# New addresses for the operands of 14,000 matmuls: odd pitches for the activations, reversed k-tiles for the weights

## The chip, the cores and the metric

One core of a Trainium2 chip runs the whole program. The metric is the time of one execution on the device in microseconds (us), lower is better. Matmuls run on TensorE (PE), whose clock the chip grants at one of two levels, 1.2 or 2.4 GHz.

## The reference, cut to what matters

Two token groups, 128 context tokens and 256 latent tokens, go through one layer of width 2048. All heavy work is a product of the 384 tokens with a weight matrix:

```python
h = rmsnorm(x, norm_mix_g) * (1 + sc_a) + sh_a
z = h @ w_in                              # 2048 x 16944: mLSTM, retention, SSD inputs and gates
merged = g0 * (y_m @ w_br_m) + g1 * (y_r @ w_br_r) + g2 * (y_s @ w_br_s)   # 1024 x 2048 each
x = x + g_a * (merged @ w_out)            # 2048 x 2048
h = rmsnorm(x, norm_mlp_g) * (1 + sc_f) + sh_f
x = x + g_f * (square(relu(h @ w_ff1)) @ w_ff2)        # 2048 x 8192, 8192 x 2048
```

The scans between the products are small beside them. Everything is fp32.

## The kernel before, in words

**Split products.** TensorE takes `float32r`, a rounded fp32. To keep fp32 precision each operand is split into a rounded half and its remainder (`hi`, `lo`), and each product is three matmuls: hi·hi, hi·lo, lo·hi. In a line of the profile such as `gb<-hlo,whi` the first name is the moving operand, which is streamed column by column, the second the stationary one, 128 columns of which are loaded into the array by an LDWEIGHTS ahead of each matmul (PEld).

**Activations.** Their halves have 16 k-tiles of 128 rows by T = 384 tokens, all in SBUF: `hhi`/`hlo` (normalised input, pool `hp`), `yhi`/`ylo` (branch outputs, 8 k-tiles, pool `hl`), `mhi`/`mlo` (merged, pool `mh`), `h2i`/`h2l` (input of the MLP, pool `h2`), `ahi`/`alo` (squared ReLU, pool `pf`). Each half is a tile of its own, and a k-tile follows the one before it at a pitch of 384 words, 1,536 bytes.

**Weights.** `strip` cuts a weight matrix into units of 512 KB. SP loads each into a `raw` tile of 128 x 1024 (6 buffers); `emit_splits` runs three units ahead (`SPB` = 3): `rnd` (ACT, L88) writes `whi`, `tt` (DVE, L91) writes `wlo`. A unit holds four k-tiles of 256 columns, or two of 512 (kind `B5`). `products` issues the matmuls (L100) in three forms: kind `A` streams the activations (384 columns) past the weights, kinds `B2` and `B5` stream the weights (256 and 512 columns) past 128-token slices of the activations. `run_units` goes through the units in order, so the order of all matmuls is fixed by the program; the 32 units of the first stage are split by `st_split` instead.

**Addresses.** In the built program `whi`, `wlo` and `raw` buffers, `hhi`, `hlo`, `h2i`, `h2l`, `mhi`, `mlo`, `yhi`, `ylo`, `ahi` and `alo` all begin 64 bytes past a multiple of 512 bytes (`whi` at 51,776, `hhi` at 76,352, `ahi` at 151,104, `yhi` at 175,168). All pitches are multiples of 512 bytes too. So in every split product the moving and the stationary operand start a multiple of 512 bytes apart. Two tiles that nothing reads, `hpad` (88 words, pool `hl`) and `fpad` (80 words, pool `pf`), take part in that. Other tiles lie otherwise: `Cb` begins 416, `W` 384 and `x2` 480 bytes past a multiple of 512.

Of the kernel before, what the change touches and what calls it, by code (L numbers as in the profile page):

```python
# [9 lines left out]
F32R = mybir.dt.float32r  # L10
# [5 lines left out]
D = 2048  # L16
T = 384
KT = D // 128
DFF = 8192
EPS = 1e-6  # L20
MQ, MK, MV, MO, MI = 0, 1024, 2048, 3072, 4096
# [25 lines left out]
def hybrid_step(ctx: ExitStack, tc: tile.TileContext, cpack, x_prompt, x_sample, c, state_mlstm_C,  # L47
# [24 lines left out]
    hp = Pool("hp")  # L72
    P = {}

    def bank(name="sb"):
        return psum([128, 512], name, bufs=4, tag="s")

    def gbank(name="gb"):
        return psum([128, 512], name, bufs=4, tag="g")
# [4 lines left out]
    def r3(ap, a):  # L84
        return ap.rearrange("p (a b) -> p a b", a=a)

    def rnd(out, in_, **kw):
        act.activation(out=out, in_=in_, func=AF.Copy, **kw)  # L88

    def tt(eng, out, a, b, op):  # L90
        eng.tensor_tensor(out=out, in0=a, in1=b, op=op)  # L91
# [7 lines left out]
    def mm(out, l, r, start=True, stop=True):  # L99
        pe.matmul(out, l, r, start=start, stop=stop)  # L100

    def tp(out, in_):
        n = in_.shape[0]
        pe.transpose(out, in_, ident[0:n, 0:n])
# [3 lines left out]
    raws, splits, done = {}, {}, set()  # L108
# [5 lines left out]
    def strip(w, c0, kt, operand, evac, kind="A", row0=0, post=None, pre=None, sync=False, hold=0):  # L114
# [3 lines left out]
        for k0 in range(0, kt, uk):  # L118
# [4 lines left out]
            if mods and tune["due"] >= 1:  # L123
                m = mods.popleft() + (tune["mx"],)
                tune["due"] -= 3 if m[2] == 7 else 1
                raw_list.append((mod_src(*m[:3]), 2))
                unit_list.append((Block("M", m, None, KT), len(raw_list) - 1, 0, 1))

    def raw_done(i):
        done.add(i)  # L130
        while pos["used"] in done:
            done.discard(pos["used"])
            pos["used"] += 1

    def emit_raws():
        while pos["raw"] < min(len(raw_list), pos["used"] + RAWB):
            src, nk = raw_list[pos["raw"]]
            t = raw_tile()
            sp.dma_start(out=r3(t, nk), in_=src)
            raws[pos["raw"]] = t  # L140
            pos["raw"] += 1

    def emit_splits(n):
        while pos["split"] < min(n, len(unit_list)):
            i = pos["split"]
            blk, ri, k0, uk = unit_list[i]
            emit_raws()
            while ri not in raws:
                pop_mods(1)
                emit_raws()  # L150
            if blk.kind != "M":
                s = raws.pop(ri)
                hi = strm([128, 1024], "whi", bufs=SPB, dt=F32R)
                lo = strm([128, 1024], "wlo", bufs=SPB, dt=F32R)
                rnd(hi, s)
                tt(dve, lo, s, hi.bitcast(F32), ALU.subtract)
                splits[i] = (r3(hi, uk), r3(lo, uk))
                raw_done(ri)
            pos["split"] += 1

# [92 lines left out]
    def K(n):  # L253
        o, s = CW[n]
        return cp[:, o:o + s] if o < CW1 else P["cr"][:, o - CW1:o - CW1 + s]
# [35 lines left out]

    cs = cst([128, KT, 32], "cs")
    pool.memset(cs, 0.0)
# [30 lines left out]
    def mod_src(m, q, r):  # L324
        o = m * D + 512 * q
        return w_mod[0, 256 * r:256 * r + 256, o:o + 512].rearrange("(k p) f -> p k f", p=128)
# [58 lines left out]
    def gf_load(q):  # L385
        if "gf" not in P:
            waiting.append(q)
            return
        ready.add(q)
        for v in range(2):  # L390
            sp.dma_start(out=P["gf"][:, v, 512 * q:512 * q + 512],
                         in_=scr_mod[1, v, 512 * q:512 * q + 512].partition_broadcast(128))

    def pop_mods(n):
        while half:
            half.pop()()
        while n and dq:
            f = dq.popleft()
            if f is None:
                break  # L400
            f()
            n -= 1
# [4 lines left out]
    rst = start([128, 3], "rst")  # L407
    acc = start([128, KT, T], "acc")
    graw = start([128, KT, 48], "graw")
    scr_g = dram([3 * KT, 128, T], "scr_g")  # L410
    junk = acc.rearrange("p k t -> p (k t)")
# [3 lines left out]
    dve.reciprocal(out=rst, in_=rst)  # L415

    scA, shA, scF, shF = (cst([128, KT, 2], n) for n in ("scA", "shA", "scF", "shF"))
    hhi = hp([128, KT, T], "hhi", dt=F32R)
    hlo = hp([128, KT, T], "hlo", dt=F32R)
    groups = [(k, 1) for k in range(4)] + [(k, 2) for k in range(4, KT, 2)]  # L420
    NG = len(groups)
    todo, mraw, wraw, wsp, mps = deque(), {}, {}, {}, {}
# [152 lines left out]
    i = 0  # L575
# [628 lines left out]
    def r_evac_v(p):  # L1204
        def f(ps):
            t = P["r"]([128, 3, 256], "vtok", bufs=2)
            src = r_tok(ps)
            for c_ in range(3):
                act.copy(out=t[:, c_], in_=src[c_])
            heads[p]["v"] = t  # L1210
            bg.append(r_scan(p))
        return f

    def r_scan(p):
# [30 lines left out]
        for hh in range(2):  # L1245
# [31 lines left out]
            for d in range(2):  # L1277
                for a, c_ in ((0, 0), (1, 1 + d)):
                    i = 2 * a + d
# [27 lines left out]
        for hh in range(2):  # L1307
            i = 2 * p + hh
# [2 lines left out]
                tp(p_[:, 128 * c_:128 * c_ + 128], o[:, hh, 128 * c_:128 * c_ + 128])  # L1311
            RR[i] = P["hl"]([128, T], "y_r", tag="ylo%d" % i)
            act.activation(out=RR[i], in_=p_[:, 0:T], func=AF.Copy, scale=gr[:, i:i + 1])
        if p == 3:
            P["hl"]([128, 88], "hpad")
        yield

    def y_split(i, src):
# [143 lines left out]
    def turn(k, p):  # L1462
        for v, a, b in GRP:
            act.activation(out=P["xa"][:, k, a:b], in_=p[:, a:b], func=AF.Copy, scale=scF[:, k, v:v + 1])
# [9 lines left out]
    def o_last(ps):  # L1474
        x2, ga, o, r = P["x2"], P["ga"], P["o"], P["r2"]
        q = slice(1536, D)
        act.activation(out=r, in_=r, func=AF.Sqrt)
        tb = [gbank(), gbank(), bank(), bank()]
        rbp = bank()
        dg = o([128, 3, 128], "dg2")  # L1480

        def close_tokens(i):
            t = o([128, 512], "to", bufs=3)
            tt(dve, t, ps[i], ga[:, min(i, 1), q], ALU.mult)
            tt(dve, x2[:, i, q], x2[:, i, q], t, ALU.add)
            act.activation(out=t, in_=x2[:, i, q], func=AF.Square, accum_out=P["sso"][:, i, 3:4])
            for j in range(4):
                tp(tb[j][:, 128 * i:128 * i + 128], x2[:, i, 1536 + 128 * j:1664 + 128 * j])

        for i in range(3):  # L1490
            close_tokens(i)
        dve.tensor_reduce(out=r, in_=P["sso"], axis=mybir.AxisListType.X, op=ALU.add)
        act.activation(out=r, in_=r, func=AF.Sqrt, scale=1.0 / D, bias=K("eps")[:, 0:1])
        dve.reciprocal(out=r, in_=r)
        for i in range(3):
            dve.tensor_scalar(out=dg[:, i], in0=ident, scalar1=r[:, i:i + 1], scalar2=None, op0=ALU.mult)
            mm(rbp[:, 128 * i:128 * i + 128], ones, dg[:, i])
        for j in range(4):
            turn(12 + j, tb[j])
        rb = o([128, T], "rb")  # L1500
        P["mh"].close()
        P["h2"] = Pool("h2", "left")
        hi = P["h2i"] = P["h2"]([128, KT, T], "h2i", dt=F32R)
        lo = P["h2l"] = P["h2"]([128, KT, T], "h2l", dt=F32R)
        xa = P["xa"]

        def make(ks):
            for k in ks:
                if k > 1 and k % 4:
                    tt(pool, xa[:, k], xa[:, k], rb, ALU.mult)  # L1510
                else:
                    tt(dve, xa[:, k], xa[:, k], rbp[:, 0:T], ALU.mult)
                for v, a, b in GRP:
                    act.activation(out=hi[:, k, a:b], in_=xa[:, k, a:b], func=AF.Identity, bias=shF[:, k, v:v + 1])  # L1514
                if k == 0:
                    act.copy(out=rb, in_=rbp[:, 0:T])
                for v, a, b in GRP:
                    dve.scalar_tensor_tensor(out=lo[:, k, a:b], in0=xa[:, k, a:b], scalar=shF[:, k, v:v + 1],  # L1518
                                             in1=hi[:, k, a:b].bitcast(F32), op0=ALU.add, op1=ALU.subtract)

        def rest():
            make(range(6, 10))
            yield
            make(range(10, 14))
            yield
            make(range(14, 16))
            o.close()
            P["f"] = Pool("pf", "right")
            P["gf"] = P["f"]([128, 2, D], "gf")
            for n in waiting:  # L1530
                gf_load(n)
            P["ahi"] = P["f"]([128, KT, T], "ahi", dt=F32R)
            P["alo"] = P["f"]([128, KT, T], "alo", dt=F32R)
            P["ssf"] = P["f"]([128, 3, 4], "ssf")
            P["rf"] = P["f"]([128, 3], "rf")
            P["f"]([128, 80], "fpad")
            dve.memset(P["rf"], 1.0)
            yield

        make(range(2))  # L1540
        emit_splits(pos["split"] + 1)
        make(range(2, 6))
        bg.append(rest())

    for n in range(4):
# [165 lines left out]
```

## Time and profile before

| what | value |
|---|---|
| time, median of 2 runs | 2836.24 us (2834.62 to 2837.87) |
| time of the profiled execution | 2840.32 us |
| its span, first to last instruction | 2838.2 us |
| mean granted TensorE clock | 0.989 of full |
| PE busy | 2760.8 us, 97% |
| DVE, ACT, POOL busy | 55%, 41%, 27% |
| DMA | 52.8% of 16 engines' span |

A matmul's own duration in the profile (338 ns for 384 columns) is a latency: the next one starts long before it ends. What counts is the time from one matmul's start to the next one's, which is read from the timeline or from the chain.

### The profile page before, as it was taken

How to read it: one execution, taken by the hardware profiler on the slowest of the kernel's cores; microseconds unless marked ns; L12 is line 12 of the kernel's file. 1: busy time of each engine (PE TensorE's matmuls, PEld its weight loads, DVE VectorE, ACT ScalarE, POOL GpSimd, SP SyncE). 2: the span in 40 equal slices, each digit the busy share in tenths (PEclk: the TensorE clock that was granted, in tenths of full speed). 3: DMA queues.
4: the chain of work that ended last, by engine and by line, in shares of the span. 5: the costliest groups of instructions: out<-in, count | busy, mean ns of one | idle time of the engine just before them, and what ended most of it. 6: DMA issues, size and time to landing. Idle time of an engine off the chain costs nothing. (4 is left out here: it accounts for less than half of the span.)

```text
span 2838.2 us, 40379 instructions
## 1 busy us (share of the span) xinstructions
PE 2760.8 (97%) x16167; PEld 2584.6 (91%) x16167; DVE 1551.8 (55%) x1871; ACT 1153.4 (41%) x1723; POOL 777.7 (27%) x608
## 2 busy tenths in 40 slices
PE   6999999999999999999999998999999999999998
PEld 5899998898999999999999877998899899889987
DVE  3666656555555445576877855873343344334434
ACT  5333444446443344444444545552233233323333
POOL 3200333422333222145676633341100110010012
PEclk9999999999999999999999999999999999999999
DMA  9955565454545445476656563664444444444443
GB/s 313 300 193 167 157 176 147 149 156 137 171 131 166 139 135 151 144 224 203 190 179 193 191 217 127 183 198 139 127 126 128 132 127 126 127 133 127 126 141 104
DMA packets 387284, 461.23 MB, mean 163 GB/s; under 512 B 19668, under 2 KB 302952, under 8 KB 385944
## 3 DMA queue, kind: packets, MB, share of 16 engines
q1 hardware_dynamic: 387096, 458.65, 52.8%
q8 instruction: 127, 2.08, 0.3%
q14 instruction: 61, 0.50, 0.1%
HBM read 446.19 MB, written 12.40 MB: 162 GB/s over the span
## 5 line engine op out<-in xcount | busy, mean ns | idle before, releaser
L91 DVE TENSOR_TENSOR wlo<-raw,whi 128x1024 fp32r<-128x1024 f32 x599 | 820.8, 1375 | 968.9 <-ACT whi L88 953.6
L88 ACT ACTIVATE whi<-raw 128x1024 fp32r<-128x1024 f32 x600 | 632.6, 1059 | 961.8 <-PE gb L100 494.5
L100 PE MATMUL gb<-hhi,whi 128*128 128x384 f32 x1600 | 555.0, 347 | 14.6 <-ACT whi L88 5.4
L100 PE MATMUL gb<-hhi,wlo 128*128 128x384 f32 x1600 | 543.5, 340 | 8.8 <-DVE wlo L91 8.7
L100 PE MATMUL gb<-hlo,whi 128*128 128x384 f32 x1600 | 541.6, 338 | 0.0
L91 POOL TENSOR_TENSOR macc<-macc,raw 128x512 f32<-128x512 f32 x206 | 352.5, 1711 | 331.8 <-issue 259.9
L100 PE MATMUL gb<-h2l,whi 128*128 128x384 f32 x1024 | 344.7, 337 | 4.6 <-DVE h2l L1518 4.5
L100 PE MATMUL gb<-h2i,whi 128*128 128x384 f32 x1024 | 344.2, 336 | 1.6 <-ACT h2i L1514 1.6
L100 PE MATMUL gb<-h2i,wlo 128*128 128x384 f32 x1024 | 343.8, 336 | 0.6 <-DVE wlo L91 0.6
L100 PEld LDWEIGHTS gb<-hhi,whi 128*128 128x128 f32 x1600 | 305.9, 191 | 29.9 <-issue 10.3
L343 DVE SCALAR_TENSOR_TENSOR macc<-raw,cs,macc 128x512 f32<-128x512 f32 x306 | 316.2, 1040 | 5.8
L100 PEld LDWEIGHTS gb<-hhi,wlo 128*128 128x128 f32 x1600 | 305.4, 191 | 12.7 <-DVE wlo L91 12.4
L100 PEld LDWEIGHTS gb<-hlo,whi 128*128 128x128 f32 x1600 | 305.4, 191 | 2.1 <-issue 1.4
L91 POOL TENSOR_TENSOR x<-x,t 128x512 f32<-128x512 f32 x45 | 71.7, 1622 | 815.9 <-DVE t L91 815.9
L100 PE MATMUL gb<-whi,hhi 128*128 128x256 f32 x768 | 222.1, 289 | 0.0
L100 PE MATMUL gb<-wlo,hhi 128*128 128x256 f32 x768 | 218.2, 284 | 3.0 <-DVE wlo L91 3.0
L100 PE MATMUL gb<-whi,hlo 128*128 128x256 f32 x768 | 218.0, 284 | 0.0
L100 PEld LDWEIGHTS gb<-h2l,whi 128*128 128x128 f32 x1024 | 193.2, 189 | 7.7 <-DVE h2l L1518 7.6
L100 PE MATMUL gb<-whi,ahi 128*128 128x512 f32 x512 | 199.3, 389 | 0.0
L100 PE MATMUL gb<-whi,alo 128*128 128x512 f32 x512 | 199.2, 389 | 0.0
L100 PE MATMUL gb<-wlo,ahi 128*128 128x512 f32 x512 | 199.2, 389 | 0.0
L100 PEld LDWEIGHTS gb<-h2i,whi 128*128 128x128 f32 x1024 | 193.5, 189 | 2.9 <-ACT h2i L1514 1.8
(407 smaller groups left out, 4153.7 us busy)
## 6 DMA issues: line engine op xcount, KB each, us to landing
raw<-in_w_in_dram SPq DMA_DIRECT2D x264, 512.0 KB
raw<-in_w_ff_dram SPq DMA_DIRECT2D x256, 512.0 KB
raw<-in_w_mod_dram SPq DMA_DIRECT2D x128, 512.0 KB
mraw<-in_w_mod_dram SPq DMA_DIRECT2D x32, 1024.0 KB
raw<-in_w_out_dram SPq DMA_DIRECT2D x32, 512.0 KB
raw<-in_w_br_r_dram SPq DMA_DIRECT2D x16, 512.0 KB
raw<-in_w_br_m_dram SPq DMA_DIRECT2D x16, 512.0 KB
raw<-in_w_br_s_dram SPq DMA_DIRECT2D x16, 512.0 KB
```

Of the source, the lines that this page charges most:

```text
L88: act.activation(out=out, in_=in_, func=AF.Copy, **kw)
L91: eng.tensor_tensor(out=out, in0=a, in1=b, op=op)
L100: pe.matmul(out, l, r, start=start, stop=stop)
L343: dve.scalar_tensor_tensor(out=macc[:, v], in0=t[:, kk], scalar=cs[:, 2 * r + kk, v:v + 1], in1=macc[:, v], op0=ALU.mult, op1=ALU.add)
```

## The change

- `hhi` and `hlo` become the two halves of one tile `hboth` whose k-tiles lie 772 words (3,088 bytes) apart; `hlo` of a k-tile begins 384 words (1,536 bytes) after its `hhi`.
- `h2i`/`h2l` and `ahi`/`alo` likewise become halves of one tile each, at a pitch of 776 words (3,104 bytes), the remainder 388 words (1,552 bytes) after the rounded half.
- `hpad` goes. That moves `yhi` and `ylo` by 352 bytes.
- In `emit_splits` the views of `whi` and `wlo` are reversed over the unit's k-tiles: k-tile 0 is written at the end of the buffer, the last one at its start. ACT's and DVE's instructions now write (and DVE reads `whi`) in four pieces of 256 words (two of 512 for `B5`) with a negative step between pieces. The products use the same views.

Nothing else changes: the matmuls, their operands' values, their order and the DMAs are the same. `mhi`, `mlo` and `fpad` stay.

```diff
+PITCH, LOW = 776, 388
...
                 hi = strm([128, 1024], "whi", bufs=SPB, dt=F32R)
                 lo = strm([128, 1024], "wlo", bufs=SPB, dt=F32R)
+                hi, lo, s = r3(hi, uk)[:, ::-1], r3(lo, uk)[:, ::-1], r3(s, uk)
                 rnd(hi, s)
                 tt(dve, lo, s, hi.bitcast(F32), ALU.subtract)
-                splits[i] = (r3(hi, uk), r3(lo, uk))
+                splits[i] = (hi, lo)
...
-    hhi = hp([128, KT, T], "hhi", dt=F32R)
-    hlo = hp([128, KT, T], "hlo", dt=F32R)
+    hboth = hp([128, KT, 772], "hboth", dt=F32R)
+    hhi, hlo = hboth[:, :, 0:T], hboth[:, :, T:2 * T]
...
-        if p == 3:
-            P["hl"]([128, 88], "hpad")
...
-        hi = P["h2i"] = P["h2"]([128, KT, T], "h2i", dt=F32R)
-        lo = P["h2l"] = P["h2"]([128, KT, T], "h2l", dt=F32R)
+        both = P["h2"]([128, KT, PITCH], "h2b", dt=F32R)
+        hi, lo = both[:, :, 0:T], both[:, :, LOW:LOW + T]
+        P["h2i"], P["h2l"] = hi, lo
...
-            P["ahi"] = P["f"]([128, KT, T], "ahi", dt=F32R)
-            P["alo"] = P["f"]([128, KT, T], "alo", dt=F32R)
+            both = P["f"]([128, KT, PITCH], "ab", dt=F32R)
+            P["ahi"], P["alo"] = both[:, :, 0:T], both[:, :, LOW:LOW + T]
```

## Rows read from the trace of the kernel before

**Rows 1.** The page: busy time by engine, and granted clock in 40 slices.
```profile
PE 2760.8 (97%) x16167; PEld 2584.6 (91%) x16167; DVE 1551.8 (55%) x1871; ACT 1153.4 (41%) x1723; POOL 777.7 (27%) x608
PEclk9999999999999999999999999999999999999999
```

**Rows 2.** Chain that ended last, 2030 to 2310 us: start, length, matmuls merged.
```profile
2037.90 135.91 PE gb L100 x780
2173.81 1.36 PE sb L100 x6
2175.17 2.72 PE gb L100 x12
2177.89 1.36 PE sb L100 x6
```

**Rows 3.** Timeline of PE near 980 us: start, length, one matmul each.
```profile
980.03 0.28 PE L100 MATMUL gb<-whi,hlo 128*128 128x256 f32 x1
...
980.99 0.28 PE L100 MATMUL gb<-wlo,hhi 128*128 128x256 f32 x1
```

**Rows 4.** Timeline of PE near 439 us.
```profile
438.31 0.53 PE L100 MATMUL gb<-hlo,whi 128*128 128x384 f32 x1
...
440.23 0.53 PE L100 MATMUL gb<-hlo,whi 128*128 128x384 f32 x1
```

**Rows 5.** Stretches: length, busy PE, PEld, DVE, ACT, POOL; PEclk, DMA share, GB/s.
```profile
2000.00:2010.00 10.00, 10.00 (x46) 8.29 (x45) 4.03 (x5) 2.74 (x3) 1.71 (x2) 1.00 0.43 135
438.60:440.50 1.90, 1.90 (x7) 1.90 (x7) 1.86 (x3) 0.06 (x1) 0.00 (x0) 0.50 1.07 370
230.00:580.00 350.00, 335.32 (x2027) 318.79 (x2026) 222.55 (x351) 154.72 (x249) 113.88 (x84) 0.98 0.53 152
```

**Rows 6.** Groups by line with shapes, PE: count, busy us, mean ns.
```profile
L100 PE MATMUL gb<-hhi,whi 128*128 128x384 f32 x1600 | 555.0, 347 | 14.6 <-ACT whi L88 5.4 <-ACT at L536 5.3 <-ACT hhi L88 3.3
L100 PE MATMUL gb<-h2l,whi 128*128 128x384 f32 x1024 | 344.7, 337 | 4.6 <-DVE h2l L1518 4.5
L100 PE MATMUL gb<-whi,hhi 128*128 128x256 f32 x768 | 222.1, 289 | 0.0
L100 PE MATMUL gb<-whi,ahi 128*128 128x512 f32 x512 | 199.3, 389 | 0.0
L100 PE MATMUL gb<-yhi,whi 128*128 128x384 f32 x384 | 128.5, 335 | 0.0
L100 PE MATMUL sb<-whi,ahi 128*128 128x512 f32 x256 | 99.6, 389 | 0.0
```

**Rows 7.** Timelines of PE where weights from other tiles are loaded next.
```profile
526.32 0.34 PE L100 MATMUL gb<-hhi,wlo 128*128 128x384 f32 x1
526.50 1.03 PE L100 MATMUL sb<-v,W 128*128 128x257 f32 x4
...
684.04 0.34 PE L100 MATMUL gb<-hhi,wlo 128*128 128x384 f32 x1
684.22 0.33 PE L100 MATMUL sb<-xd,Cb 128*128 128x64 f32 x2
...
1707.66 0.39 PE L100 MATMUL sb<-whi,mlo 128*128 128x512 f32 x1
1707.89 0.27 PE L104 MATMUL sb<-cp,x 128*128 128x128 f32 x1
```

**Rows 8.** Groups by line with shapes, DVE and ACT: the splits and a comparison.
```profile
L91 DVE TENSOR_TENSOR wlo<-raw,whi 128x1024 fp32r<-128x1024 f32 x599 | 820.8, 1375 | 968.9 <-ACT whi L88 953.6 <-DMA raw<-in_w_out_dram 7.1 <-DMA raw<-in_w_in_dram 4.0
L91 DVE TENSOR_TENSOR Cb<-Cb,cbm 128x1024 f32<-128x1024 f32 x12 | 15.1, 1258 | 0.0
L88 ACT ACTIVATE whi<-raw 128x1024 fp32r<-128x1024 f32 x600 | 632.6, 1059 | 961.8 <-PE gb L100 494.5 <-PE sb L100 375.3 <-issue 36.2
```

**Rows 9.** Who waited for whom, PE alone: us in total, times, longest us.
```profile
PE gb L100 <- DVE wlo L91: 17.5, 20, 1.9
PE gb L100 <- DVE h2l L1518: 4.5, 5, 1.8
```

## The prediction, made before the changed kernel was run

> **What bounds the kernel now.** I read the page first. PE is busy 97% of the span and its clock is at the full level in every slice [rows 1]. So time can only come from what a matmul costs. The second view is the chain that ended last, because its pieces give start-to-start times over many matmuls. In the last unbroken first-MLP stage 780 matmuls take 135.91 us; 12 of them have 512 columns, and 18 of those take 4.08 us, so 226.7 ns each; the 768 with 384 columns then take (135.91 - 12 x 0.2267) / 768 = 173.4 ns each [rows 2]. In the timeline, eight matmuls of 256 columns take 0.96 us, 120 ns each [rows 3].
>
> At 2.4 GHz and one column per cycle, 384, 256 and 512 columns take 160.0, 106.7 and 213.3 ns. So every split product costs 13.3 ns more than its stream, whatever its width, and whichever pool its activations lie in: `h2` and `hhi` and `ahi` lie in different places and give the same excess. I next looked where the clock was at its lower level, 1.2 GHz (granted 0.50 from 438.6 to 440.5 us) [rows 5]: six matmuls of 384 columns take 1.92 us there, 320 ns each, and 384 / 1.2 is 320 [rows 4]. The excess is gone. So the 13.3 ns are not a fixed cost of a matmul. Something cannot keep up with a full-speed stream, and what runs beside each stream is the load of the next matmul's weights.
>
> The touched matmuls, three products to each row: 3 x (1600 + 768) on `hhi`/`hlo` = 7,104; 3 x 1024 on `h2` = 3,072; 3 x (512 + 256) on `ahi`/`alo` = 2,304; 3 x 384 on `yhi`/`ylo` = 1,152 [rows 6]. Together 13,632, whose excess is 13,632 x 13.3 = 181 us. This is the only stock from which new addresses can win.
>
> **The change part by part.** *Addresses of the products.* In the kernel before, moving and stationary operand always lie a multiple of 512 bytes apart. After it, the distance modulo 512 is 16k bytes on `hboth`, 32k on the rounded halves and 32k + 16 on the remainders of `h2` and `ahi`, and 352 on `yhi`/`ylo`. The matmuls keep their columns and their count. The trace of before has no split product with any other distance. The nearest rows are split products during which the weights of another tile are loaded, ahead of a plain fp32 matmul: from `W`, 192 bytes off (modulo 512), from `Cb`, 160 off, from `x2`, 96 off. They take 0.18, 0.18 and 0.23 us [rows 7]. Without any excess they would be 0.160, 0.160 and 0.213. So three other distances don't remove the excess; within the view's grain of 0.01 us they leave it or add some: 0.18 - 0.1734 = 6.6 ns, 0.23 - 0.2267 = 3.3 ns. All three are multiples of 32 bytes; an odd multiple of 16 is in no row. The bounds of this term are thus from -181 us (all excess gone) to 13,632 x 6.6 = +90 us. I take 0, since the three rows lie next to the excess of before and none lies near the bare stream.
>
> The same excess in every row and no excess at half clock also fit a load that takes its share of one path into the array each time, whatever the addresses. And the times are the same whether DVE and ACT are busy 40% and 27% [rows 5] or not: other engines' reads and writes, whose addresses run through all distances, leave no mark on 768 matmuls in a row [rows 2].
>
> Here the Trainium skill can be weighed against the trace. "TensorE: Matmul & The Clock Gate", in "Step-by-step: what each phase is for", gives PE two independent read ports, one for the stream and one for the weights. By that no address matters, and the change is worth 0 us. But the same page, under "Wait — 56ns, not 53.3ns?", puts the floor between two warm matmuls at some 2.5 ns; the trace shows 13.3. If the change brought the matmuls down to that floor, the sum would be 13,632 x 10.8 = 147 us less, an estimate from that page. The trace does not say which of the two holds for an odd distance.
>
> *The reversed split.* 568 units (600 less the 32 of the first stage) get an ACT and a DVE instruction in pieces. DVE's product on `Cb`, whose mask is read in eight pieces per instruction, takes 1,258 ns on the mean, the split 1,375 [rows 8]. So pieces cost nothing visible there; below nothing the bound is the same row, 117 ns a unit, 66 us of DVE work off the path. ACT has no such row; the bound above is as much again, 1,059 ns. What hides either is the matmul work of a unit: 24 x 173.4 = 4.2 us, with three units of lead. Should both double, DVE would do 568 x 1.4 us more, 781 us, and ACT 602; in the densest stretch, 230 to 580 us, 350 / 4.2 = 83 units would lift DVE from 223 to 337 of 350 us [rows 5]. Only there would PE begin to wait on `wlo`, on which it waits 17.5 us in the whole span now [rows 9]. I take 0.
>
> *Shared tiles.* An instruction still writes one k-tile of one half. Matmuls read k-tiles of `h2i` while later ones are still being written, with 4.5 us of waiting on `h2l` in total [rows 9], so waits go by region and not by tile, and two halves in one tile add no wait. Were it by tile, those few us would grow by some us once, at the start of each stage. No DMA, queue or semaphore step moves. The pads and pools only shift addresses.
>
> **The sum.** Profiled execution 2840.3 us, change 0. The median of the runs shown is 4.1 us lower, so the forecast is 2836 us. A measurement of this kernel can tell about 2% from no change, 57 us.
>
> **The rivals.**
> *A collision between reads (faster).* Stream and weight load are read at the same time from the same memory. If they collide when both lie on lines of the same parity, 16 bytes a line, and in no other case, the excess falls away where the distance is an odd multiple of 16: half of `hboth` (odd k), 3,552; the `lo` third of `h2`, 1,024; that of `ahi`, 768. That is 5,344 x 13.3 = 71 us: 2769 by the profiled execution, 2765 by the median. For it: the excess is exactly constant where the distance is, and vanishes at half clock. Against it: in this case it needs a distance the trace doesn't have, and 96, 160 and 192 bytes show the excess.
> *The same, wider.* If only a distance of 0 modulo 512 collides, it stays for k = 0 alone: 12,964 matmuls escape, 172 us, 2664 by the median. The three rows speak against that; only that they load for plain fp32 matmuls leaves it open.
> *Slower.* A stream or load that starts off a 64-byte boundary needs one more fetch. In the kernel before no split product does. Afterwards it is three quarters of `hboth` (5,328), two thirds of `h2` (2,048) and of `ahi` (1,536), and all of `yhi`/`ylo` (1,152): 10,064. At the 3.3 ns of the `x2` row that is 33 us, 2869 by the median; at the 6.6 ns of `Cb`, 66 us, 2903. `x2` and `Cb` begin 32 bytes off such a boundary, which speaks for it; `W` begins on one and reads 0.18 too, which speaks against it. From 5.6 ns on it is over 2%.
> *The change does what it says only in form*: every address moves, and nothing depends on it. That is the forecast.
>
> **How the numbers follow.** Forecast (within 15 us of 2836): 0.60. Parity collision: 0.17, 2765, with some spread. Wider collision: 0.10, 2664. Slower: 0.13, of which 0.06 is over 2%. The range holds the forecast, most of the parity case (from 2745 if a little more than odd multiples escape) and the slower case up to 2885: about 0.60 + 0.14 + 0.09 = 0.83. Its own range for the likeliest case is 2825 to 2850. Faster by over 2%: 0.17 + 0.10, less the part of the parity case that falls short of 57 us, so 0.25. Slower by over 2%: 0.06. Within: 0.69.
>
> **What would show it.** In the changed profile, the piece of the chain for the first-MLP stage should again be close to 136 us for 780 matmuls, and a 512-column unit 4.08 us. If reads collide, k-tiles differ: matmuls on odd k of `hboth`, or on `h2l` and `alo`, would start 160 ns and 213 ns apart and the rest 173 and 227. If a boundary costs, `yhi` and `ylo` matmuls, all 32 bytes off, would all be a few ns longer. The split instructions should stay near 1.06 and 1.38 us, and PE's waits on `wlo` near 17 us. The prediction is wrong if an odd multiple of 16 bytes is special, which no row here could show.

## The result, and the profile of the changed kernel

| | before | changed |
|---|---|---|
| median of the runs | 2836.24 us (2834.62 to 2837.87) | 2856.43 us (2855.93 to 2856.93) |
| profiled execution | 2840.32 us, span 2838.2 us | 2855.93 us, span 2854.1 us |
| mean granted clock | 0.989 | 0.992 |

The ratio on record is 1.0068, 95% interval 1.0051 to 1.0084 (it is not exactly the quotient of the two medians, here or below): a small loss of about 20 us, where nothing was forecast. In the changed kernel all line numbers are one higher: the products stand at L101, the splits at L89 and L92.

The page, busy time and granted clock, to be read beside [rows 1]:

```profile
PE 2778.2 (97%) x16167; PEld 2591.8 (91%) x16167; DVE 1549.4 (54%) x1871; ACT 1152.7 (40%) x1723; POOL 777.3 (27%) x608
PEclk9999999999999999999999999999999999999999
```

The counts and the clock's digits are the same, and the mean granted clock is no lower, but PE is busy 17.4 us longer. So the loss lies in what a matmul costs. The chain that ended last, 2030 to 2310 us, shows it; the piece of 780 is the first-MLP stage of [rows 2], the rest of the rows is the second-MLP stage and the start of the next:

```profile
2040.80 137.49 PE gb L101 x780
2178.30 1.39 PE sb L101 x6
2179.69 2.79 PE gb L101 x12
2182.47 1.40 PE sb L101 x6
2183.87 2.81 PE gb L101 x12
...
2308.86 21.21 PE gb L101 x121
```

In the chain of the kernel before, the stage after that begins with this row:

```profile
2301.65 28.45 PE gb L100 x164
```

The 780 matmuls take 137.49 us instead of 135.91, 1.58 us or 2 ns each more. Where a unit of 18 products with 512 columns took 4.08 us every time, they now take 1.39 + 2.79 = 4.18 and 1.40 + 2.81 = 4.21 us: they cost more, and not all the same. From the first row of the stage to the start of the next it is 2308.86 - 2040.80 = 268.06 us, before 2301.65 - 2037.90 = 263.75 (the start of the x780 piece is in [rows 2]). That is 4.3 us more; there are four such pairs of stages, so some 17 us.

The timelines of PE, first in the branch products with `yhi`/`ylo`, which now all lie 352 bytes away; then with 256 columns, beside [rows 3]; then at half clock, beside [rows 4], with the view by windows under it (granted clock 0.50):

```profile
1242.70 0.34 PE L101 MATMUL gb<-ylo,whi 128*128 128x384 f32 x1
...
1245.88 0.34 PE L101 MATMUL gb<-ylo,whi 128*128 128x384 f32 x1
...
977.73 0.28 PE L101 MATMUL gb<-wlo,hboth 128*128 128x256 f32 x1
...
983.80 0.28 PE L101 MATMUL gb<-wlo,hboth 128*128 128x256 f32 x1
...
438.14 0.52 PE L101 MATMUL gb<-hboth,wlo 128*128 128x384 f32 x1
...
439.10 0.52 PE L101 MATMUL gb<-hboth,wlo 128*128 128x384 f32 x1
```

```profile
438.20:440.00 1.80, 1.80 (x7) 1.80 (x6) 1.80 (x3) 0.00 (x0) 0.00 (x0) 0.50 0.84 269
```

18 products of `y` from 1242.70 to 1245.88 us take 176.7 ns each. The same products in the kernel before took 173.3 ns, 21 from the first row to the last:

```profile
1257.43 0.33 PE L100 MATMUL gb<-yhi,wlo 128*128 128x384 f32 x1
...
1261.07 0.33 PE L100 MATMUL gb<-yhi,wlo 128*128 128x384 f32 x1
```

51 products of 256 columns take 6.07 us, 119.0 ns each, a nanosecond less than before. At half clock three products take 0.96 us, 320 ns each, which is their bare stream, as before. So do 70 products of this trace that ran at half clock without a stall, at ten distances from 0 to 144 bytes.

The splits in the groups by line, beside [rows 8], and after them PE's waits, beside [rows 9]:

```profile
L92 DVE TENSOR_TENSOR wlo<-raw,whi 128x1024 fp32r<-128x1024 f32 x599 | 815.6, 1367 | 987.4 <-ACT whi L89 982.9 <-DMA macc<-in_b_mod_dram 3.2
L89 ACT ACTIVATE whi<-raw 128x1024 fp32r<-128x1024 f32 x600 | 632.6, 1059 | 987.8 <-PE gb L101 500.5
```

```profile
PE gb L101 <- DVE wlo L92: 16.7, 18, 1.9
PE gb L101 <- DVE h2b L1519: 4.5, 5, 1.8
```

In pieces and backwards, the splits take 1,367 and 1,059 ns, where they took 1,375 and 1,059, and PE waits no longer for them. None of the loss is there.

**The whole trace.** Since all starts of matmuls are in the trace and all addresses in the built program, the excess over the bare stream can be averaged for every kind of product (start to next start, less columns / 2.4 GHz; more than 45 ns counts as a stall and is left out, and so is the first 84 us). For each I also took the distance from the operand that streams to the weights that are loaded next. In the kernel before that distance is 0 modulo 512 throughout.

```
kind, columns              matmuls  excess ns: before  changed   difference us
ahi/alo, 512                  2304             13.40    18.15       +10.9
hhi/hlo, 384                 ~4400             13.69    15.21        +6.7
h2, 384                      ~3035             13.38    15.40        +6.1
yhi/ylo, 384                  1145             13.34    16.62        +3.8
hhi/hlo, 256                 ~2210             13.19    11.51        -3.7
mhi/mlo, 512 (not moved)       540             14.30    14.35         0.0
```

The sum is +23.8 us, against 20.2 us between the medians. In the two profiled executions the last matmul comes 15.8 us later; there 5.4 us less went to half-clock stretches, 2.4 us less to stalls and 0.8 us less to the other matmuls of the changed kernel, which closes the sum to within a microsecond.

### The profile page after: what moved, and what is told of

It is laid out like the page before. It is cut to its first block, busy times and chain, and to the rows that moved or that the text cites. A ratio compares the mean times of both kernels' runs of the same rounds, so it can differ in the third digit from the quotient of the medians.

```text
span 2854.1 us, 40379 instructions
## 1 busy us (share of the span) xinstructions
PE 2778.2 (97%) x16167; PEld 2591.8 (91%) x16167; DVE 1549.4 (54%) x1871; ACT 1152.7 (40%) x1723; POOL 777.3 (27%) x608
## 5 line engine op out<-in xcount | busy, mean ns | idle before, releaser
L92 DVE TENSOR_TENSOR wlo<-raw,whi 128x1024 fp32r<-128x1024 f32 x599 | 815.6, 1367 | 987.4 <-ACT whi L89 982.9
L89 ACT ACTIVATE whi<-raw 128x1024 fp32r<-128x1024 f32 x600 | 632.6, 1059 | 987.8 <-PE gb L101 500.5
L101 PE MATMUL gb<-hboth,whi 128*128 128x384 f32 x3200 | 841.9, 344 | 14.2 <-ACT at L538 5.2
L101 PEld LDWEIGHTS gb<-hboth,whi 128*128 128x128 f32 x3200 | 582.7, 190 | 31.6 <-issue 12.0
L101 PE MATMUL gb<-hboth,wlo 128*128 128x384 f32 x1600 | 544.9, 341 | 8.5 <-DVE wlo L92 8.5
L101 PE MATMUL gb<-h2b,whi 128*128 128x384 f32 x2048 | 529.9, 339 | 6.2 <-DVE h2b L1519 4.5
L92 POOL TENSOR_TENSOR macc<-macc,raw 128x512 f32<-128x512 f32 x206 | 352.7, 1712 | 333.5 <-issue 258.3
L101 PEld LDWEIGHTS gb<-h2b,whi 128*128 128x128 f32 x2048 | 374.4, 189 | 10.6 <-DVE h2b L1519 7.6
L101 PE MATMUL gb<-h2b,wlo 128*128 128x384 f32 x1024 | 347.6, 339 | 0.3 <-DVE wlo L92 0.3
L101 PE MATMUL gb<-whi,ab 128*128 128x512 f32 x1024 | 340.6, 394 | 0.0
L101 PEld LDWEIGHTS gb<-hboth,wlo 128*128 128x128 f32 x1600 | 304.3, 190 | 11.8 <-DVE wlo L92 11.7
L92 POOL TENSOR_TENSOR x<-x,t 128x512 f32<-128x512 f32 x45 | 71.8, 1624 | 830.5 <-DVE t L92 830.5
L101 PE MATMUL gb<-whi,hboth 128*128 128x256 f32 x1536 | 283.3, 283 | 0.0
L101 PEld LDWEIGHTS gb<-whi,hboth 128*128 128x128 f32 x1536 | 238.2, 188 | 3.9 <-issue 3.2
L101 PEld LDWEIGHTS gb<-whi,ab 128*128 128x128 f32 x1024 | 192.2, 188 | 46.0 <-issue 0.8
L101 PE MATMUL gb<-wlo,hboth 128*128 128x256 f32 x768 | 216.1, 281 | 3.0 <-DVE wlo L92 3.0
L101 PE MATMUL gb<-wlo,ab 128*128 128x512 f32 x512 | 201.7, 394 | 0.0
L101 PEld LDWEIGHTS gb<-h2b,wlo 128*128 128x128 f32 x1024 | 193.4, 189 | 0.8 <-DVE wlo L92 0.8
L101 PE MATMUL sb<-whi,ab 128*128 128x512 f32 x512 | 180.2, 393 | 0.0
L101 PEld LDWEIGHTS gb<-wlo,hboth 128*128 128x128 f32 x768 | 144.6, 188 | 3.9 <-DVE wlo L92 3.6
```

## The experiments

Theories: (A) the split in pieces costs ACT, DVE or their readers something; (B) a stream that begins off a 64-byte boundary costs more, wherever the weights are; (C) the odd pitch itself, a distance that changes from k-tile to k-tile; (D) the distance between stream and weights decides, and 0, where the kernel before stood, is a good value for some widths. Pads are tiles that nothing reads; they change addresses alone. Of each experiment the edit to the kernel before is shown, unless said otherwise.

**1. The reversed split alone.**

```diff
+                hi, lo, s = r3(hi, uk)[:, ::-1], r3(lo, uk)[:, ::-1], r3(s, uk)
                 rnd(hi, s)
                 tt(dve, lo, s, hi.bitcast(F32), ALU.subtract)
-                splits[i] = (r3(hi, uk), r3(lo, uk))
+                splits[i] = (hi, lo)
```

> The kernel before with the reversed split alone; all pitches and pads as before, so every split product again has its two operands a multiple of 512 bytes apart. Theory (a matmul's excess over its stream is set by the distance between the streamed operand and the weights being loaded, modulo a few hundred bytes): no change, 2836 us, 120, 173.4 and 226.7 ns from start to start. Rival (the instructions in four pieces with a negative step cost ACT, DVE or the reads of PE time): slower by up to the whole 20 us, 2856.

Measured: 2837.48 us against 2836.56, ratio 1.0004 (0.9994 to 1.0013). Its first-MLP piece in the chain is that of before, to the hundredth:

```profile
2037.32 135.91 PE gb L100 x780
```

**2. The changed kernel with the split forwards again** (the edit to the changed kernel):

```diff
-                hi, lo, s = r3(hi, uk)[:, ::-1], r3(lo, uk)[:, ::-1], r3(s, uk)
...
-                splits[i] = (hi, lo)
+                splits[i] = (r3(hi, uk), r3(lo, uk))
```

> The changed kernel without the reversed split; odd pitches, shared tiles and the missing pad stay. Distances modulo 1024 (four k-tiles) are those of the changed kernel. Theory: still slower than before, 2846 to 2866 us, by the second MLP product above all. Rival (the reversal costs): 2836.

Measured: 2857.95 us, ratio 1.0078 (1.0062 to 1.0093). The chain has the longer pieces of the changed kernel:

```profile
2046.70 137.49 PE gb L101 x780
2184.19 1.39 PE sb L101 x6
2185.59 2.79 PE gb L101 x12
```

The two together: the reversal costs nothing and gives nothing that these runs can tell, the pitches and the missing pad cost all of the 20 us. (A) falls.

**3. Everything moved by 32 bytes, distances kept.**

```diff
+    cst([128, 8], "cpad")
...
-            P["hl"]([128, 88], "hpad")
+            P["hl"]([128, 80], "hpad")
...
-            P["f"]([128, 80], "fpad")
+            P["f"]([128, 72], "fpad")
```

> The kernel before with 32 bytes put ahead of every operand of the split products (one small unused tile more in the first pool, 32 bytes less in hpad and fpad). All distances stay a multiple of 512 bytes, but every operand now begins 32 bytes off a 64-byte boundary. Theory (distance): 2836 us, excess 13.3 ns everywhere. Rival (starts off a 64-byte boundary cost a fetch): all 13,632 products pay; at the 2 ns each that 20 us over 10,064 products would mean, 27 us more, 2863.

Measured: 2839.24 us, ratio 1.0003 (0.9994 to 1.0012). Now every stream and every weight begins 32 bytes off a 64-byte boundary, and a first-MLP stage is the same again:

```profile
2036.71 135.91 PE gb L100 x780
2172.62 1.36 PE sb L100 x6
2173.98 2.72 PE gb L100 x12
```

(B) falls: what lies off a 64-byte boundary costs nothing as long as the distances stay.

**4. All activations 64 bytes further from the weights, old pitches.** `spad` lies between the weight buffers and everything behind them.

```diff
+    strm([128, 16], "spad")
...
-            P["hl"]([128, 88], "hpad")
+            P["hl"]([128, 72], "hpad")
...
-            P["f"]([128, 80], "fpad")
+            P["f"]([128, 64], "fpad")
```

> The kernel before with all activations 64 bytes further from the weights (64 bytes of pad after the weight buffers, hpad and fpad 64 bytes shorter). Pitches, tiles and split as before, so the distance is the same for every k: +64 modulo 512 where activations are streamed, -64 (192 modulo 256) where weights are streamed. Theory (distance): products of 256 columns gain, about 8 ns of excess instead of 13.3 as at that distance in the changed kernel (12 us in the Q, K, V strips of mLSTM and retention), 384 columns 13 to 16 ns, 512 columns 12 to 17; in all 2825 to 2855 us, and the excess differs from 13.3 ns in at least one of the three widths. Rivals (64-byte boundary; or odd pitches break a run of reads): nothing changes, 2836 us, 13.3 ns in all three.

Measured: 2840.29 us, ratio 1.0013 (1.0004 to 1.0023), and under that calm total two large terms of opposite sign. The end of a first-MLP stage and the second-MLP stage in the chain:

```profile
2029.99 132.10 PE gb L100 x758
2162.09 1.40 PE sb L100 x6
2163.49 2.80 PE gb L100 x12
2166.29 1.40 PE sb L100 x6
2167.69 2.80 PE gb L100 x12
```

18 products take 4.20 us, 233.3 ns each, an excess of 20.0 ns, in every unit. With 384 columns the excess stays at 13.3 (in the first row 12 of the 758 have 512 columns, which leaves 173.3 ns for each of the others), with 256 it falls to 7.8 (means over the trace). By the counts: 2,301 x 6.6 + 540 x 5.7 = +18.3 us for 512 columns, 2,200 x 5.4 = -11.9 us for 256, -1.6 for 384: +4.8 us; measured +3.7. No k-tile has another distance than its neighbour here, so (C) isn't needed for such terms; (D) is borne out, and the distance acts differently on each width. The fall of the 256 columns was expected, the 20.0 ns with 512 columns were not (12 to 17).

**5. The odd pitch for `ahi`/`alo` alone.**

```diff
-            P["ahi"] = P["f"]([128, KT, T], "ahi", dt=F32R)
-            P["alo"] = P["f"]([128, KT, T], "alo", dt=F32R)
+            both = P["f"]([128, KT, 776], "ab", dt=F32R)
+            P["ahi"], P["alo"] = both[:, :, 0:T], both[:, :, 388:388 + T]
```

> The kernel before with the shared tile and odd pitch for ahi and alo alone. Theory (distance, costs add up by stage): the 2,304 products of 512 columns of the second MLP product go from 13.4 to 18.2 ns of excess as in the changed kernel, 11 us, 2847 us; all other products stay at 13.4. Rival (the 20 us come from somewhere else, such as a first stall that the rest inherits): no change, 2836, or all 20.

Measured: 2848.03 us against 2835.40, ratio 1.0048 (1.0031 to 1.0065). In the chain the first MLP product is that of before within 0.02 us, and the second is that of the changed kernel, piece by piece:

```profile
2037.24 135.93 PE gb L100 x780
2173.17 1.39 PE sb L100 x6
2174.56 2.79 PE gb L100 x12
2177.35 1.40 PE sb L100 x6
2178.75 2.81 PE gb L100 x12
```

The mean excess with 512 columns is 18.16 ns, 11 us in all, the other kinds keep theirs. So the loss adds up stage by stage, and about half of it is in this one.

**6 to 8. Three sets of constant distances**, a different one for each pool, to see whether the distance modulo 256 tells the excess whichever tiles are read. One run each; the edits differ in their pads alone (words of `spad`, `hpad`, `mpad`, `h2pad`, `fpad`: 32, 48, 16, 40, 48; then 48, 32, 24, 56, 40; then 8, 40, 16, 48, 24). The first:

```diff
+    strm([128, 32], "spad")
...
-            P["hl"]([128, 88], "hpad")
+            P["hl"]([128, 48], "hpad")
...
+        P["mh"]([128, 16], "mpad")
...
+        P["h2"]([128, 40], "h2pad")
...
-            P["f"]([128, 80], "fpad")
+            P["f"]([128, 48], "fpad")
```

> Constant distances, one per pool, by pads (modulo 256, streamed operand minus weights being loaded): 384 columns at 128 (hhi), 160 (yhi), 32 (h2); 256 columns at 128; 512 columns at 64 (mhi), 128 (ahi). Theory (distance alone): excesses near those of the changed kernel at these distances: 16 to 18, 15, 14 to 15 ns; 12.5; 14 and 22. At 64 the 512 columns are cheaper than at 192 (20 ns in the run with all distances at 64). Rival (only a pitch that changes the distance from k to k costs): 13.3 ns in all of them.

> As the run before, 384 columns at 192 (hhi), 224 (yhi), 160 (h2); 256 columns at 64; 512 columns at 224 (mhi), 96 (ahi). Theory: 14 to 17, 15 to 17, 15 ns; 11; 19 and 20; and the 384 columns at 160 on h2 like those at 160 on yhi in the run before, within 1 ns. Rival (the pool decides): the two differ, or all are at 13.3.

> As the run before, 384 columns at 32 (hhi), 192 (yhi), 224 (h2); 256 columns at 224; 512 columns at 160 (mhi), 32 (ahi). Theory: 14 to 15, 14 to 17, 15 to 17 ns; 12 to 13; 19 and 14 to 15; each 384 value like that of the same distance on another pool in the two runs before, within 1 ns. Rival (the pool decides): they differ, or all are at 13.3.

Measured: 2860.05, 2855.45 and 2857.25 us against 2835.40. Mean excess, with the distance modulo 256 behind the @:

```
             e6             e7             e8
hhi 384   15.9 @128      15.0 @192      14.2 @32
h2  384   15.5 @32       14.5 @160      13.4 @224
y   384   14.1 @160      13.6 @224      16.2 @192
hhi 256   12.1 @128      10.3 @64       11.7 @224
a   512   19.3 @128      20.0 @96       20.0 @32
m   512   15.7 @64       20.0 @224      20.9 @160
```

In different pools 160 gives 14.5 and 14.1, 224 gives 13.4 and 13.6; that agrees. But 192 gives 15.0 and 16.2, and 32 gives 14.2 and 15.5, further apart than the 1 ns expected; and 512 columns at 32, expected at 14 to 15 ns, have 20.0. So the distance modulo 256 tells the excess of 384 columns to 1 or 2 ns, and is not the whole rule. With 512 columns nothing beats 0. With 384 columns none is below 13.3, where before had 13.3 to 13.7. With 256 columns every one of them is below it.

**9. Distance 16 everywhere: the parity rival of the prediction.** Both halves in one tile, sliced from word 4 on (shown for `hhi`; likewise `mhi`, `h2i`, `ahi`; `hpad` 80 and `fpad` 72, which puts `y` at 32).

```diff
-    hhi = hp([128, KT, T], "hhi", dt=F32R)
-    hlo = hp([128, KT, T], "hlo", dt=F32R)
+    hb_ = hp([128, 2 * KT * T + 8], "hhl", dt=F32R)
+    hhi, hlo = r3(hb_[:, 4:4 + KT * T], KT), r3(hb_[:, 4 + KT * T:4 + 2 * KT * T], KT)
```

> The kernel before with hhi/hlo, mhi/mlo, h2i/h2l and ahi/alo all begun 16 bytes later, hi and lo alike, pitches as before (yhi/ylo 32 bytes later): a constant odd multiple of 16. Rival of the prediction (reads collide only on lines of the same parity): the excess of the 12,480 products moved by 16 goes, 13.3 ns each, 166 us, about 2670 us. Theory (each distance has its own excess, near the means of the changed kernel): 384 columns 14.6 to 15 ns, 256 columns 11 to 12, 512 columns 16; about 2845 us.

Measured, one run: 2853.01 us against 2837.51, slower than the 2845 expected. The first-MLP piece is as long as in the changed kernel:

```profile
2045.72 137.55 PE gb L100 x780
```

At an odd multiple of 16, 384 columns have an excess of 15.5 ns, 512 columns 15.0 (`a`) and 18.8 (`m`), 256 columns 11.7; `y`, at 32, has 13.3, where 32 gave 14.2 and 15.5 in experiments 8 and 6. `a` and `m` are 3.8 ns apart at one distance, so from one pool to another the distance can miss by that much. Had the excess gone, this kernel would have been over 150 us faster. The parity rival falls.

**10. Distance 64 for `hhi`/`hlo` and `y` alone, a multiple of 256 for the rest**: what the table so far says is best for each width.

```diff
+    strm([128, 16], "spad")
...
-            P["hl"]([128, 88], "hpad")
+            P["hl"]([128, 72], "hpad")
...
+        P["mh"]([128, 48], "mpad")
...
+        P["h2"]([128, 48], "h2pad")
```

> The kernel before with hhi/hlo (and yhi/ylo) 64 bytes further from the weights, and mhi/mlo and h2i/h2l brought back to a multiple of 512 by pads of their own; split, pitches and tiles as before. Theory (distance): 256 columns fall to 7.8 ns of excess and 384 columns stay at 13.3, as in the run with all distances at 64, and the 512 columns stay at 13.4: 2,304 x 5.4 = 12 us less, 2824 us, a ratio of 0.996. Rival (a pool's address, not the distance, made the 256 columns cheap there, or the gain is given back in waits): 2836.

Measured: 2824.46 us against 2837.51, ratio 0.9952 (0.9938 to 0.9966). This is half a percent faster than the kernel before, and faster than the changed one too. The pads put `h2` and `mhi`/`mlo` 64 + 192 = 256 bytes further on, so not at a multiple of 512 as expected; their excess is that of before all the same (13.4 and 14.3 ns). The timeline near 980 us, to be read beside [rows 3], and its second-MLP pieces in the chain, beside [rows 2]:

```profile
979.35 0.28 PE L100 MATMUL gb<-whi,hlo 128*128 128x256 f32 x1
...
982.07 0.28 PE L100 MATMUL gb<-whi,hlo 128*128 128x256 f32 x1
```

```profile
2158.70 1.36 PE sb L100 x6
2160.06 2.72 PE gb L100 x12
2162.78 1.36 PE sb L100 x6
```

24 products of 256 columns take 2.72 us, 113.3 ns each instead of 120, and 18 of 512 columns 4.08 us as before. Over the trace the 256-column excess falls from 13.2 to 7.8 ns: 2,210 x 5.4 = 12 us, of the 13 measured. The stretch from 936 to 1110 us in the view by windows, whose second number in brackets counts matmuls, first of the kernel before, then changed, then this one:

```profile
936.00:1110.00 174.00, 174.00 (x1442) 171.20 (x1442) 91.01 (x128) 69.02 (x127) 42.70 (x58) 1.00 0.47 139
```

```profile
936.00:1110.00 174.00, 174.00 (x1455) 171.19 (x1454) 94.73 (x133) 69.16 (x126) 42.68 (x58) 1.00 0.47 140
```

```profile
936.00:1110.00 174.00, 174.00 (x1480) 171.15 (x1479) 96.88 (x134) 71.24 (x127) 41.05 (x56) 1.00 0.50 147
```

PE shows as busy all the time in all three; only the count tells that more work is done in the same time.

**11. Only `hlo` and `alo` moved by 64.** Does the load that runs beside the stream decide alone (the narrow form of D)? Then of the three products of a k-tile only the one that has `lo` loaded next should change.

```diff
+    hp([128, 16], "lpad")
     hlo = hp([128, KT, T], "hlo", dt=F32R)
...
+            P["f"]([128, 16], "apad")
             P["alo"] = P["f"]([128, KT, T], "alo", dt=F32R)
...
-            P["hl"]([128, 88], "hpad")
+            P["hl"]([128, 72], "hpad")
...
-            P["f"]([128, 80], "fpad")
+            P["f"]([128, 64], "fpad")
```

> The kernel before with alo alone, and hlo alone, 64 bytes further on (yhi/ylo too, which costs nothing at 64). In the second MLP product the three matmuls of a k-tile stream whi past ahi, wlo past ahi, whi past alo; the loads during them are those of the next matmul: ahi, alo, ahi. Theory in its narrow form (the distance to the weights being loaded during the stream counts): only wlo past ahi goes to 20 ns of excess, the other two stay at 13.4; in the 256-column products only wlo past hhi falls to 8 ns. Rival (the distance to the matmul's own weights counts): whi past alo goes to 20 and whi past hlo to 8, the others stay. Together the two changes cancel to about 1 us, 2837 us.

Measured, one run: 2844.85 us against 2837.33, where the two changes were expected to cancel.

```
512 columns, excess ns: whi past ahi 15.0 | wlo past ahi, alo loaded next 15.8 | whi past alo 22.4
256 columns, excess ns: whi past hhi 11.0 | wlo past hhi, hlo loaded next 11.0 | whi past hlo 11.8
```

All three change, and with 512 columns the one whose own weights are the moved ones changes most, not the one beside whose stream they are loaded. So the narrow form falls, and its rival with it, by which the others would have stayed. `whi` past `ahi` has both its own weights and those loaded next at distance 0, and yet 15.0 ns instead of 13.3; only its neighbours lie otherwise. The same shows with 384 columns: 64 throughout costs 13.3 ns (experiment 4), 0 throughout 13.7, but here, with `hlo` at 64 and `hhi` at 0, `hhi` past `wlo` has 15.0. Which of the reads of neighbouring matmuls meet each other stays open.

## Why the prediction was wrong

**The bound and the stock held.** The time moved by what a matmul costs; 13,632 products were touched, and it is their start-to-start times that changed.

**The step that failed: the term of the addresses, set to 0.** The prediction took 0 "since the three rows lie next to the excess of before and none lies near the bare stream", and held that the excess fits a load that takes its share of one path "whatever the addresses". Experiments 1 and 2 put the whole loss on the pitches and the missing pad, experiment 5 about half of it on one pitch; experiment 3 shows that a common shift off the 64-byte boundary costs nothing, and experiment 4 that a constant distance moves 512 columns from 13.4 to 20.0 ns, 256 from 13.2 to 7.8, and leaves 384 where they were. So the term is not 0: it depends on how the operands lie to each other, and on the width. It came out at +23.8 us, inside the bounds of -181 and +90, made up of +27.5 on 384 and 512 columns and -3.7 on 256.

Two steps of the reasoning led there. First, the excess was the same in all pools of the kernel before, and I read that as independence of the address. But all pools stood at distance 0 modulo 512, so those rows could not tell. What the rows did say of other distances was [rows 7], with 3.3 and 6.6 ns more; a plain fp32 matmul came next there, and the grain of the view is 10 ns. They were the right hint, and I rounded it to nothing. The starts in the trace are finer than the view: over the 9, 6 and 13 places without a stall where `W`, `Cb` and `x` are loaded next after 384, 384 and 512 columns, the mean excess is 17.6, 17.3 and 17.7 ns, in all three some 4 ns above the 13.4 of before. Second, I looked for a place where the excess vanishes, and asked only whether the change would reach it. The kernel before sat at 13.3 to 13.7 ns with 384 and at 13.4 with 512 columns (`ahi`/`alo`), which no other distance that was tried beats on the mean by more than 0.4; a pitch that runs through many distances then averages over worse ones. In the second MLP product of the changed kernel the means by distance run from 12.4 to 27.5 ns, against a constant 13.4 before. Only the 256 columns stood at a poor place, and they gained.

The mechanism itself, within this: in that stage the distance to the weights loaded next, modulo 256, accounts for 52% of the spread, that to the matmul's own weights for 41%, the two together for 62%. Modulo 4,096 the first accounts for 96%, but that makes 144 groups, which nearly name the place in the program as well. The address of the stream alone, modulo any power of two up to 16,384, accounts for 1% at most. Nor does one distance cost the same in a walking pitch as in a constant one: at 0 the mean there is 17.6 ns, against 13.4 before, at 32 it is 14.6, against 20.0 in experiment 8. So the neighbours' distances count too, and what share is due to a distance that changes (C) stays open. That a collision of reads is behind it fits that the excess depends on two addresses and vanishes at half clock, with the new pitches too. That is argued, not shown: no run saw the reads themselves.

The Trainium skill, cited in the prediction for its two independent read ports ("TensorE: Matmul & The Clock Gate", "Step-by-step: what each phase is for"), says in the same place that a load of the next weights takes no read bandwidth from the running matmul. By that alone experiment 4 should have shown no change with any width; it showed +6.6 and -5.4 ns, so it matters here where the two lie. The measurement decides; whether it is bandwidth that is lost, no run shows.

**What was right.** The reversed split: 0 forecast, 1.0004 measured, with splits of 1,059 and 1,367 ns. Shared tiles: 0 forecast, and PE's wait on the second half of `h2` is 4.5 us as before. No excess at half clock. What the prediction said of the noise was too wide: it took 2% as what a measurement can tell from no change, while the two runs of each kernel agree within 0.2%, and the loss of 0.7% is clear of that.

**The rivals.** The parity rival fell in experiment 9, the wider collision with it and with experiment 4 (13.3 ns left at a distance of 64 in 384 columns). The slower rival had the right sign, and its marker, `y` a few ns longer throughout, came true with 3.3 ns; its mechanism is wrong all the same, since in experiment 3 all streams are off a 64-byte boundary and nothing is longer. A marker that two mechanisms share proves neither.

## What to carry to other kernels

Where matmuls with alternating weight loads take longer than their stream, the distance between streamed and stationary operand is worth some runs with nothing but pads: they cost a few bytes, and here the best setting found gave 0.5%. Choose it for each width by itself, keep it constant over the k-tiles, and measure it in the kernel itself, since a distance did not cost the same in every pool. The pitches that walked through the distances here were worse on the mean than a constant 0 with 384 and 512 columns. And when a quantity is constant in a profile, ask first whether what it might depend on was varied there at all.

## What was not expected of the hardware

- The excess of a split product at full clock depends on how far apart streams and weights lie, its neighbours' too, and by width: at a constant distance of 64 bytes (192 where the weights stream) 13.3 ns for 384 columns, 7.8 for 256 and 20.0 for 512; at 0 it is 13.3 to 13.7, 13.2 and 13.4 (`mhi`/`mlo` 14.3).
- Where both operands moved together by 32 bytes (experiment 3) its means did not change by 0.1 ns.
- At half clock products of 384 columns take 320 ns, the bare stream, at all ten distances that occurred there in the changed kernel: the excess is absent.
- ACT and DVE write four pieces with a negative step in 1,059 and 1,367 ns, as fast as one piece (1,059 and 1,375).
